# Attention with the probabilities as the stationary operand, V's two parts and a column of ones moving

## The chip, the cores and the metric

The kernel runs on one core of one Trainium2 chip. The metric is the device time of one execution in microseconds (us); shorter is better. Engines are named as in the profile: PE is TensorE's matmul, PEld its weight load (the load of the stationary operand), DVE is VectorE, ACT is ScalarE, POOL is GpSimd, SP issues most DMAs.

## The reference

Two layers of an encoder trunk run on a prompt of 1024 tokens and on a running stream of 32 tokens (float32, model width 1024). Layer 0 is forgetting attention with 16 heads of 64 features, layer 1 a gated linear recurrence; each is followed by a squared-ReLU MLP of 4096 hidden features. The part that matters here is the attention of the prompt:

```python
def fox_attend(q, k, v, cq, ck, qpos, kpos):
    logits = jnp.einsum('bqhd,bkhd->bhqk', q, k).astype(jnp.float32) * FOX_SCALE
    bias = jnp.swapaxes(cq, 1, 2)[..., :, None] - jnp.swapaxes(ck, 1, 2)[..., None, :]
    mask = kpos[None, :] <= qpos[:, None]
    logits = jnp.where(mask, logits + bias, -jnp.inf)
    p = jax.nn.softmax(logits, axis=-1).astype(v.dtype)
    return jnp.einsum('bhqk,bkhd->bqhd', p, v)
```

The mask is causal, so of the 8 x 8 blocks of 128 queries and 128 keys 36 are computed per head. The result is multiplied by a sigmoid gate and projected.

## The kernel before

Activations lie with features on partitions and tokens along the free axis, in three chunks of 352 tokens. Products keep float32 accuracy by splitting each operand exactly into a high and a low float32r part and adding three of the four products (`mm3`, line 152).

Heads are worked in eight pairs. For each pair `fox` (lines 639 to 648) calls `fox_attend` and then the projections of the next pair: V (`pj`, 72 matmuls of 352 columns), K, then `rest`, which turns V and K back to tokens on partitions (`to`, line 767), projects Q and writes the operands of the next attention. The tiles `vT`, `kh`, `qh` (features of a pair) and `KA`, `KB`, `QA`, `QX`, `VH`, `VL` (operands of the two heads) exist once, so each waits until the pair before has let go of it.

`fox_attend` has two parts. First, for both heads, the row maxima: 20 matmuls `mp` per head (line 835), each reduced by DVE (lines 840 and 843); the maxima are turned (`mt`, line 848) and go by DMA into a row of `QX`. Then per head, for two chunks of 512 queries and for each block of 128 keys: the logits `st` with keys on partitions and queries along the free axis (lines 866, 867; up to 512 columns), `pf` = exp on ACT (869), the causal triangle on POOL (871, on diagonal blocks), the high part `ph` on POOL (875), the low part `pl` on DVE (876), and three matmuls into `pv` (878 to 880) with a block of V stationary and the probabilities moving. `VH` holds V's high part in 64 columns and ones in the other 64, so that rows 64 to 127 of `pv` are the softmax's sums; `VL` holds the low part and zeros. ACT makes 1/sum by Ln and Exp, DVE multiplies, and the result, which has features on partitions, goes to DRAM.

The order of the work is made when the program is built: a list scheduler with a model of the engines places each instruction, and every engine then runs its own list in that order. The order of allocation binds it: of PSUM, tag A (projections, two banks), B (logits and maxima, three), E (`pv`, two) and D (one bank, for all that is turned on PE, `mt` and `to` among it) are handed on from tile to tile in the order of the program text.

Of the kernel before, what the change touches and what calls it, by code (L numbers as in the profile page):

```python
# [16 lines left out]
D = 1024  # L17
# [12 lines left out]
FMIN = 1e-15  # L30
TABLE = "natural_log_exp_and_others"


def consts():
# [11 lines left out]
    # pairs of key s and query t: in one block of four, then in the two halves of larger blocks  # L46
# [13 lines left out]
class K:  # L60
# [21 lines left out]
    def gains(self):  # L82
        # gains, features of a tile on partitions: loaded in rows, turned on the tensor engine
# [9 lines left out]
    # constants that the first products do not need  # L93
# [11 lines left out]
    # what frees PSUM goes ahead of other work  # L105
# [3 lines left out]
    # an order of two instructions on one engine  # L109
# [11 lines left out]
    # one unit of weights: [128, X, Y] with X*Y = 1024, split exactly into two float32r parts  # L121
# [29 lines left out]
    # out += W^T x over the given k tiles; each product in three float32r passes  # L151
# [12 lines left out]
    # per token of a chunk, tokens on partitions in three columns (the last one overlaps the  # L164
    # second): sums over all features of s, [128, C]
# [8 lines left out]
    # such columns as rows along the free axis, the same on every partition  # L174
# [7 lines left out]
    # running sum over feature tiles of y ** 2: [128, C], features of a tile on partitions  # L182
# [13 lines left out]
    # r = (ss / n + eps) ** -0.5  # L196
    def rsqrt(self, r, ss, n, pool):
# [9 lines left out]
        # one Newton step  # L207
# [13 lines left out]
    # x * gain in split form; y is scratch  # L221
# [13 lines left out]
    # the norm's factor per token, which the products take on later: as columns, or as rows  # L235
    def prestat(self, x, y, rows):
# [13 lines left out]
        # the product's factor is the square, which the norm after it takes to the square again  # L250
# [4 lines left out]
    # the norm's factor per token of y * sc, for y; ss the sums of y ** 2  # L255
# [14 lines left out]
    # x += rmsnorm(y * sc), sc a factor per token, acc the sum of y ** 2; y is overwritten  # L270
# [52 lines left out]
    # the last chunk of the output is normed with tokens on partitions, in three blocks (the last  # L323
    # one overlaps the second). Ahead of that: x in that form, and the gains on diagonals
# [43 lines left out]
    # one token chunk of the input: loaded with tokens on partitions,  # L368
# [11 lines left out]
    # brought to features on partitions, with the first norm's factor per token,  # L380
    def start_turn(self, n, pool, xts, tags):
# [36 lines left out]
    # normed and split  # L418
# [14 lines left out]
    # mixer's output (features on partitions, split, per token chunk) -> W_out -> norms ->  # L433
    # squared-ReLU MLP -> norms; returns the next layer's h, or writes the outputs
    def tail(self, os, w_out, layer, rs=None, after=None):
# [5 lines left out]
        with ExitStack() as c:  # L441
# [10 lines left out]
            # output projection  # L452
# [3 lines left out]
            # a factor of the norm before the products is less urgent than the next chunk's norms  # L456
# [24 lines left out]
            # MLP, G tiles of the hidden layer at a time  # L481
# [27 lines left out]
            # one output tile of the second matrix, over the given hidden tiles  # L509
# [27 lines left out]
            # the first three tiles of the hidden layer token chunk by token chunk, as the norms finish  # L537
# [25 lines left out]
            # the last two groups token chunk by token chunk, so that the norms overlap the products;  # L563
            # the last group's second weights in an h tile that is free by then
# [27 lines left out]
    # forgetting attention; returns its gated output  # L592
    def fox(self):
# [7 lines left out]
        with ExitStack() as c:  # L601
# [3 lines left out]
            # the input, token chunk by token chunk, with the first products on each  # L605
# [5 lines left out]
            tags = ("QA0", "QA1", "QX0", "QX1", "KA0", "KA1", "KB0", "KB1", "VH0", "VH1", "VL0", "VL1")  # L611
# [40 lines left out]
    # the forget gates of one token chunk: heads on partitions, tokens along the free axis  # L652
# [13 lines left out]
    def fox_setup(self, pool, psp, lf):  # L666
# [13 lines left out]
        # -cumulative sums; the scan runs on -logf  # L680
# [13 lines left out]
        # the same for the running streams, behind their cache  # L694
# [9 lines left out]
        # persistent operands of the two heads of a pair; rows 64.. carry the bias terms  # L704
# [4 lines left out]
        z64 = pool.tile([128, 64], F32, name="z64")  # L709
        self.v.memset(z64, 0.0)  # L710
        self.KA, self.KB, self.QA, self.QX, self.VH, self.VL = [], [], [], [], [], []
        for h in range(2):
            mk = lambda nm: pool.tile([128, SEQ], F32R, name=f"{nm}{h}", tag=f"{nm}{h}", bufs=1)
            ka, kb, qa, qx, vh, vl = (mk(nm) for nm in ("KA", "KB", "QA", "QX", "VH", "VL"))
            vh, vl = (t.rearrange("p (b f) -> p b f", b=8) for t in (vh, vl))
# [5 lines left out]
            self.VH.append(vh); self.VL.append(vl)  # L721

    # projections of one pair of heads: features on partitions
    def fox_pair(self, pool, psp, hs, w_in, p):
# [34 lines left out]
        def tok_out(src, dst_p, dst_s, keep):  # L759
            # back to tokens on partitions  # L760
# [18 lines left out]
        def keep_v(b0, tk):  # L779
            if b0 == 8:  # L780
                return
            for h in range(2):
                hi, lo = self.VH[h], self.VL[h]
                f = slice(64 * h, 64 * h + 64)
                self.v.tensor_copy(hi[:, b0:b0 + 4, 0:64], tk[:, :, f])
                self.v.tensor_tensor(lo[:, b0:b0 + 4, 0:64], tk[:, :, f], hi[:, b0:b0 + 4, 0:64].bitcast(F32), op=ALU.subtract)
# [34 lines left out]
    def fox_attend(self, pool, psp, p, cur, od):  # L821
        nc = self.nc
        qh = cur
        for h in range(2):
            r = slice(64 * h, 64 * h + 64)
            head = 2 * p + h
            ka, kb, qa, qx, vh, vl = self.KA[h], self.KB[h], self.QA[h], self.QX[h], self.VH[h], self.VL[h]
            # row maxima of the biased logits
# [23 lines left out]
            self.v.tensor_tensor(qx[0:64], qh[r, 0:SEQ], qa[r].bitcast(F32), op=ALU.subtract)  # L852
        for h in range(2):
            r = slice(64 * h, 64 * h + 64)
            head = 2 * p + h
            ka, kb, qa, qx, vh, vl = self.KA[h], self.KB[h], self.QA[h], self.QX[h], self.VH[h], self.VL[h]
            for c in range(2):
                pv = psp.tile([128, 512], F32, name=f"pv{head}_{c}", tag="E", bufs=2)
                nkb = 4 * c + 4
                for b in range(nkb):  # L860
                    q0 = max(512 * c, 128 * b)
                    N = 512 * c + 512 - q0
# [3 lines left out]
                    nc.tensor.matmul(ps[:, :N], lhsT=ka[:, kk], rhs=qa[:, q0:q0 + N], start=True, stop=False)  # L866
                    nc.tensor.matmul(ps[:, :N], lhsT=kb[0:97, kk], rhs=qx[0:97, q0:q0 + N], start=False, stop=True)  # L867
                    pf = pool.tile([128, 512], F32, name=f"pf{u}", tag="pf", bufs=3)
                    self.s.activation(pf[:, :N], ps[:, :N], AF.Exp, bias=self.ncol[:, b, head:head + 1])  # L869
                    if b >= 4 * c:  # L870
# [6 lines left out]
                    o = pv[:, q0 - 512 * c:]  # L877
# [441 lines left out]
```

## Time and profile before

| | |
|---|---|
| time, three runs | 2998.22 to 3001.53 us, median 3000.46 us |
| span of the profiled execution | 2996.0 us |
| PE busy over the span | 2942.2 us (98%), 18511 matmuls |
| PEld busy | 2855.2 us (95%) |
| DVE, ACT, POOL busy | 1734.0, 934.1, 967.0 us (58%, 31%, 32%) |
| first and last `pv` matmul | 136.2 and 682.2 us |

The execution that was profiled has no time of its own on record beside its span; the median of the runs is 4.5 us above the span, and this is taken as what lies around it. A busy time counts from an instruction's start to its modelled end; matmuls overlap, so 200 busy matmuls of 0.4 us can take far less than 80 us. The granted clock of TensorE is shown in tenths of full speed (9 stands for 90% or more) and is 9 in all 40 slices.

### The profile page before, as it was taken

What the parts mean: (1) busy time and instruction counts of PE and PEld (TensorE: products, weight loads), DVE (VectorE), ACT (ScalarE), POOL (GpSimd) and SP (SyncE); (2) the same over time, 40 slices, a digit from 0 to 9 for tenths busy, and PEclk for the clock granted to TensorE, in tenths of its full rate; (3) what the DMA queues carried; (4) which work ended last, traced back from release to release, by engine and by line L of the source; (5) the groups of instructions that cost most, each with busy time, mean ns of one, the idle gap of its engine ahead of it and who ended that gap; (6) DMA issues with size and microseconds to landing.
All of it is one profiled execution on the core that took longest, in us unless ns stands there. A gap on an engine that the chain in (4) does not pass through costs nothing.

```text
span 2996.0 us, 46448 instructions
## 1 busy us (share of the span) xinstructions
PE 2942.2 (98%) x18511; PEld 2855.2 (95%) x18511; DVE 1734.0 (58%) x2980; ACT 934.1 (31%) x1915; POOL 967.0 (32%) x1151
## 2 busy tenths in 40 slices
PE   7999999999999999999998999999999999999999
PEld 6888888899999999999997999999999999999998
DVE  6788888874544444445468656654474454454545
ACT  5455555555432111111133122212353111111112
POOL 3345444531432112121145444433362121121223
PEclk9999999999999999999999999999999999999999
DMA  5221121134321111121122111104432111111112
GB/s 152 62 52 44 48 53 48 51 112 147 106 74 57 43 43 50 36 57 49 37 82 95 35 59 41 47 27 120 140 118 76 36 57 43 43 50 36 57 61 69
DMA packets 217817, 195.59 MB, mean 65 GB/s; under 512 B 14312, under 2 KB 193648, under 8 KB 217472
## 3 DMA queue, kind: packets, MB, share of 16 engines
q1 hardware_dynamic: 216576, 192.49, 21.5%
q8 instruction: 145, 2.38, 0.3%
q14 instruction: 72, 0.59, 0.1%
q0 software_dynamic: 1024, 0.13, 0.0%
HBM read 147.00 MB, written 45.52 MB: 64 GB/s over the span
## 4 chain that ended last, share of the span: by engine, by line
PE 89%; DVE 5%; issue 1%; POOL 1%; ACT 1%; DMA 1%; SPq 0%; DVEq 0%; POOLq 0%; ACTq 0%
PE up L158 24%; PE dn L158 24%; PE hj L158 8%; PE pj L158 8%; PE gp L158 6%; PE po L158 5%; PE lv L1166 1%; PE ss L753 1%; PE pv L880 1%; PE pv L879 1%; PE pv L878 1%; PE st L867 1%; PE st L866 1%; PE mp L835 1%; PE lv L1181 1%
## 5 line engine op out<-in xcount | busy, mean ns | idle before, releaser
L520 DVE TENSOR_TENSOR ya<-dn,ya 128x352 f32<-128x352 f32 x672 | 348.3, 522 | 550.4 <-PE dn L158 550.4
L162 POOL TENSOR_TENSOR rl<-rl 128x352 f32<-128x352 f32 x192 | 190.2, 999 | 1031.7 <-ACT uh L501 1029.3
L145 DVE TENSOR_TENSOR wl<-wr,wh 128x1024 fp32r<-128x1024 f32 x203 | 280.4, 1382 | 147.0 <-ACT wh L142 84.6
L158 PE MATMUL dn<-uh,wl 128*128 128x352 f32 x1440 | 356.9, 323 | 0.0
L158 PE MATMUL dn<-uh,wh 128*128 128x352 f32 x1440 | 353.7, 324 | 2.5 <-DVE ya L520 2.5
L158 PE MATMUL dn<-ul,wh 128*128 128x352 f32 x1440 | 353.5, 323 | 0.0
L499 ACT ACTIVATE rl<-up 128x352 f32<-128x352 f32 x192 | 88.8, 463 | 783.1 <-PE up L158 712.8
L158 PE MATMUL up<-hh,wl 128*128 128x352 f32 x1536 | 291.5, 323 | 0.0
L158 PE MATMUL up<-hh,wh 128*128 128x352 f32 x1536 | 287.5, 323 | 2.1 <-ACT wh L142 1.7
L158 PE MATMUL up<-hl,wh 128*128 128x352 f32 x1536 | 288.1, 323 | 0.0
L158 PEld LDWEIGHTS up<-hh,wh 128*128 128x128 f32 x1536 | 253.5, 188 | 3.1 <-ACT wh L142 2.3
L158 PEld LDWEIGHTS dn<-uh,wh 128*128 128x128 f32 x1440 | 251.3, 188 | 4.4 <-DVE ya L520 4.4
L158 PEld LDWEIGHTS up<-hh,wl 128*128 128x128 f32 x1536 | 254.4, 188 | 0.0
L158 PEld LDWEIGHTS up<-hl,wh 128*128 128x128 f32 x1536 | 254.1, 188 | 0.0
L158 PEld LDWEIGHTS dn<-uh,wl 128*128 128x128 f32 x1440 | 252.6, 188 | 0.0
L158 PEld LDWEIGHTS dn<-ul,wh 128*128 128x128 f32 x1440 | 251.8, 188 | 0.0
L144 POOL TENSOR_SCALAR wh<-wr 128x1024 fp32r<-128x1024 f32 x109 | 120.8, 1108 | 294.3 <-PE pj L158 93.0
L503 DVE TENSOR_TENSOR ul<-rl,uh 128x352 fp32r<-128x352 f32 x192 | 142.6, 754 | 124.9 <-POOL rl L162 124.8
L142 ACT CAST wh<-wr 128x1024 fp32r<-128x1024 f32 x94 | 98.7, 1050 | 347.2 <-PE up L158 221.5
L876 DVE TENSOR_TENSOR pl<-pf,ph 128x512 fp32r<-128x512 f32 x192 | 124.5, 652 | 59.9 <-POOL ph L875 34.7
L875 POOL TENSOR_SCALAR ph<-pf 128x512 fp32r<-128x512 f32 x192 | 125.2, 654 | 51.6 <-PE pv L879 24.7
L869 ACT ACTIVATE pf<-st,ncol 128x512 f32<-128x512 f32 x192 | 109.7, 578 | 71.2 <-PE st L867 40.1
(343 smaller groups left out, 5673.0 us busy)
## 6 DMA issues: line engine op xcount, KB each, us to landing
wr<-in_ffn_w_up_dram SPq DMA_DIRECT2D x64, 512.0 KB, 4.0
wr<-in_ffn_w_down_dram SPq DMA_DIRECT2D x64, 512.0 KB, 3.8
wr<-in_fox_w_in_dram SPq DMA_DIRECT2D x32, 512.0 KB, 4.1
wr<-in_hgrn_w_in_dram SPq DMA_DIRECT2D x32, 512.0 KB, 4.1
x<-xd SPq DMA_DIRECT2D x22, 704.0 KB, 4.9
xd<-x SPq DMA_DIRECT2D x18, 704.0 KB, 3.1
out_dram<-tk SPq DMA_DIRECT2D x32, 256.0 KB, 2.4
odg<-go SPq DMA_DIRECT2D x30, 176.0 KB, 2.5
```

The source lines that it names most:

```text
L142: self.s.copy(wh, raw)
L144: self.g.tensor_scalar(out=wh, in0=raw, scalar1=1.0, scalar2=0.0, op0=ALU.mult, op1=ALU.add)
L145: self.v.tensor_tensor(wl, raw, wh.bitcast(F32), op=ALU.subtract)
L158: self.nc.tensor.matmul(ps, lhsT=ws[kk][a], rhs=xs[kk][b], start=i == 0, stop=i == tot - 1)
L162: self.g.tensor_tensor(out, a, b, op=op)
L499: self.s.activation(rl, ps[:, :C], AF.Relu)
L503: self.v.tensor_tensor(ul, rl, uh.bitcast(F32), op=ALU.subtract)
L520: self.v.tensor_tensor(ys[n][:, o], ps[:, :C], ys[n][:, o], op=ALU.add)
L753: nc.tensor.matmul(ss[:, :C], lhsT=self.blk, rhs=sq, start=True, stop=True)
L869: self.s.activation(pf[:, :N], ps[:, :N], AF.Exp, bias=self.ncol[:, b, head:head + 1])
L875: self.g.tensor_scalar(out=ph[:, :N], in0=pf[:, :N], scalar1=1.0, scalar2=0.0, op0=ALU.mult, op1=ALU.add)
L876: self.v.tensor_tensor(pl[:, :N], pf[:, :N], ph[:, :N].bitcast(F32), op=ALU.subtract)
```

## The change

The product of probabilities and V is turned round: a 128 x 128 block of probabilities is stationary and V moves. One tile `VV` per head holds, for each block of keys, V's low part (64 columns), its high part (64) and two columns of ones. `ph` meets all 130 columns, `pl` the last 66; the output `pv` has queries on partitions, three blocks of queries side by side in one bank. The queries are therefore taken in three chunks of 3, 3 and 2 blocks in place of two of 4, so `st`, `pf`, `ph` and `pl` have at most 384 columns. Per chunk DVE takes the reciprocal of the ones column, ACT copies the low columns out, DVE adds the high ones and multiplies into `oq` (two buffers, by the pair's parity). When the second head of a pair is far enough, eight blocks of `oq` are turned on PE (`ot`, PSUM tag D), copied by ACT and sent to DRAM. The Ln and Exp of the sums and the tile of zeros are gone. The rest of the difference is comments and line numbers.

```diff
+VW = 130
...
-                jk = pool.tile([128, 512], F32, name=f"jk{t0}_{hf}", tag="w", bufs=1)
+                jk = pool.tile([128, 512], F32, name=f"jk{t0}_{hf}", tag="oT", bufs=2)
...
-            tags = ("QA0", "QA1", "QX0", "QX1", "KA0", "KA1", "KB0", "KB1", "VH0", "VH1", "VL0", "VL1")
+            tags = ("QA0", "QA1", "QX0", "QX1", "KA0", "KA1", "KB0", "KB1", "VV0", "VV1", "oq0", "oq1")
...
-            self.g.tensor_copy(vh[:, :, 64:128], self.ones[:, None, 0:64].to_broadcast([128, 8, 64]))
-            self.g.tensor_copy(vl[:, :, 64:128], z64[:, None, :].to_broadcast([128, 8, 64]))
...
+            vv = pool.tile([128, 8, VW], F32R, name=f"VV{h}", tag=f"VV{h}", bufs=1)
...
+            self.g.tensor_copy(vv[:, :, 128:VW], self.ones[:, None, 0:VW - 128].to_broadcast([128, 8, VW - 128]))
...
+        oq = pool.tile([128, 8, 128], F32, name=f"oq{p}", tag=f"oq{p % 2}", bufs=1)
         for h in range(2):
...
-            for c in range(2):
-                nkb = 4 * c + 4
-                for b in range(nkb):
+            for c0, c1 in ((0, 3), (3, 6), (6, 8)):
...
+                pv = pv[:, 0:3 * VW].rearrange("p (i f) -> p i f", f=VW)
+                for b in range(c1):
...
-                    nc.tensor.matmul(o, lhsT=vh[:, b], rhs=ph[:, :N], start=b == 0, stop=False)
-                    nc.tensor.matmul(o, lhsT=vl[:, b], rhs=ph[:, :N], start=False, stop=False)
-                    nc.tensor.matmul(o, lhsT=vh[:, b], rhs=pl[:, :N], start=False, stop=b == nkb - 1)
...
-                self.s.activation(w[r], pv[64:128], AF.Ln)
-                self.s.activation(w[r], w[r], AF.Exp, scale=-1.0)
...
-                self.v.tensor_tensor(oT[r], pv[0:64], w[r], op=ALU.mult)
-                nc.sync.dma_start(od[p][r, qc], oT[r])
+                    for t, f0 in ((ph, 0), (pl, 64)):
+                        for i in range(q0, c1):
+                            nc.tensor.matmul(pv[:, i - c0, f0:VW], lhsT=t[:, (i - q0) * 128:(i - q0) * 128 + 128],
+                                             rhs=vv[:, b, f0:], start=b == f0 == 0 and i == c0,
+                                             stop=b == i or b == f0 == 0, skip_group_check=b + f0 > 0 or i > c0)
...
+                self.v.reciprocal(rc, pv[:, 0:nq, 128])
...
+                with self.soon():
+                    self.s.copy(lo, pv[:, 0:nq, 0:64])
+                    self.v.tensor_tensor(lo, pv[:, 0:nq, 64:128], lo, op=ALU.add)
+                self.v.tensor_tensor(oq[:, c0:c1, r], lo, rc[:, :, None].to_broadcast([128, nq, 64]), op=ALU.mult)
+                if h and c0:
+                    a, b = (0, 4) if c0 == 3 else (4, 8)
+                    ps = psp.tile([128, 512], F32, name=f"ot{u}", tag="D", bufs=1)
+                    for i in range(a, b):
+                        nc.tensor.transpose(ps[:, (i - a) * 128:(i - a) * 128 + 128], oq[:, i], self.ident)
...
+                    self.s.copy(oT, ps)
+                    nc.sync.dma_start(od[p][:, a * 128:b * 128], oT)
```

Two places on PE show what becomes of the order. In a name the first number counts: `pv3_0` is head 3 (the second of pair 1) and the chunk of queries that starts at 0, `vT2` belongs to pair 2; a number after that is the tile's own. The first place is the start of head 3's product. Before:

```order
L878 MATMUL pv3_0_2244<-ph232_2251,VH1_864 128x512
L879 MATMUL pv3_0_2244<-ph232_2251,VL1_865 128x512
L753 MATMUL ss274_2763<-sq274_2760,mats_261 128x352
L158 MATMUL pj351_3272<-hh7_227,wh350_3268 128x352 x8
L158 MATMUL pj351_3272<-hh7_227,wl350_3269 128x352 x4
L880 MATMUL pv3_0_2244<-pl232_2252,VH1_864 128x512
L866 MATMUL st238_2316<-QA1_862,KA1_860 128x512
L867 MATMUL st238_2316<-QX1_863,KB1_861 128x512
```

And now, at the same head:

```order
L882 MATMUL pv3_0_2520<-VV1_860,ph241_2527 128x130 x3
L882 MATMUL pv3_0_2520<-VV1_860,pl241_2528 128x66 x3
L868 MATMUL st246_2600<-QA1_858,KA1_856 128x384
L869 MATMUL st246_2600<-QX1_859,KB1_857 128x384
L882 MATMUL pv3_0_2520<-VV1_860,ph242_2543 128x130 x2
L882 MATMUL pv3_0_2520<-VV1_860,pl242_2544 128x66 x2
L868 MATMUL st247_2615<-QA1_858,KA1_856 128x384
L869 MATMUL st247_2615<-QX1_859,KB1_857 128x384
```

Three matmuls of 512 columns became six of 130 and 66, and the projections (`pj`, of pair 3's V) that stood between the steps of this head before are not there now.

The second place is the end of the same head, where the maxima of pair 2 begin. Before:

```order
L880 MATMUL pv3_1_2303<-pl244_2398,VH1_864 128x128
L767 MATMUL to276_2773<-ident_70,kh2_2411 128x128 x2
L835 MATMUL mp290_2832<-KB0_851,QX0_853 128x512
L158 MATMUL pj353_3324<-hh39_664,wh350_3268 128x352 x3
L158 MATMUL pj353_3324<-hl39_665,wh350_3268 128x352 x3
L835 MATMUL mp291_2835<-KB0_851,QX0_853 128x128
L158 MATMUL pj353_3324<-hl39_665,wh350_3268 128x352 x5
L158 MATMUL pj355_3356<-hh7_227,wh354_3352 128x352 x2
L835 MATMUL mp293_2839<-KB0_851,QX0_853 128x512
L158 MATMUL pj355_3356<-hh7_227,wh354_3352 128x352 x6
```

Now:

```order
L898 MATMUL ot257_2782<-ident_70,oq1_2265 128x128 x2
L833 MATMUL mp311_3235<-KB0_849,QX0_851 128x512
L833 MATMUL mp312_3238<-KB0_849,QX0_851 128x512
L833 MATMUL mp314_3253<-KB1_857,QX1_859 128x128
L765 MATMUL to272_3000<-ident_70,vT2_2790 128x128 x4
L833 MATMUL mp316_3257<-KB1_857,QX1_859 128x256
L833 MATMUL mp318_3262<-KB1_857,QX1_859 128x384
L765 MATMUL to274_3012<-ident_70,vT2_2790 128x128 x4
L833 MATMUL mp320_3267<-KB1_857,QX1_859 128x512
L765 MATMUL to276_3024<-ident_70,vT2_2790 32x128
L833 MATMUL mp322_3272<-KB1_857,QX1_859 128x512
L159 MATMUL pj371_3897<-hh39_664,wh368_3841 128x352 x8
```

Before, the turning of `vT2` lay far ahead of this point, at the start of pair 1's attention. Now it comes after `ot`, whose bank D it needs, and the next projection `pj371` (the last third of pair 3's V) comes after that, since `vT` exists once.

## Rows read from the trace of the kernel before

**Rows 1.** The page: PE's share of the span, and the chain that ended last.

```profile
PE 2942.2 (98%) x18511; PEld 2855.2 (95%) x18511; DVE 1734.0 (58%) x2980; ACT 934.1 (31%) x1915; POOL 967.0 (32%) x1151
PE 89%; DVE 5%; issue 1%; POOL 1%; ACT 1%; DMA 1%; SPq 0%; DVEq 0%; POOLq 0%; ACTq 0%
```

**Rows 2.** Busy time by engine, 120 to 640 us: PE, PEld, DVE, ACT, POOL, clock, DMA.

```profile
120.00:640.00 520.00, 513.25 (x2941) 463.25 (x2939) 432.64 (x939) 277.22 (x558) 237.47 (x397) 1.00 0.21 55
```

**Rows 3.** Groups by shape, 100 to 690 us, line 878: count | busy, mean ns.

```profile
L878 PE MATMUL pv<-ph,VH 128*128 128x512 f32 x96 | 38.5, 401 | 1.3 <-POOL ph L875 1.3
L878 PE MATMUL pv<-ph,VH 128*128 128x384 f32 x32 | 10.8, 338 | 0.0
L878 PE MATMUL pv<-ph,VH 128*128 128x256 f32 x32 | 8.9, 279 | 0.0
L878 PE MATMUL pv<-ph,VH 128*128 128x128 f32 x32 | 7.5, 235 | 0.0
```

**Rows 4.** Timeline of weight loads, 133.5 to 135.3 us: start, duration, what.

```profile
133.75 0.19 PEld L867 LDWEIGHTS st<-QX,KB 97*128 97x128 f32 x1
133.93 0.69 PEld L158 LDWEIGHTS pj<-hl,wh 128*128 128x128 f32 x4
...
134.86 0.19 PEld L866 LDWEIGHTS st<-QA,KA 128*128 128x128 f32 x1
134.98 0.19 PEld L867 LDWEIGHTS st<-QX,KB 97*128 97x128 f32 x1
135.09 0.19 PEld L866 LDWEIGHTS st<-QA,KA 128*128 128x128 f32 x1
135.21 0.19 PEld L867 LDWEIGHTS st<-QX,KB 97*128 97x128 f32 x1
```

**Rows 5.** The same, 306.9 to 308.2 us.

```profile
307.13 0.19 PEld L879 LDWEIGHTS pv<-ph,VL 128*128 128x128 f32 x1
307.36 0.19 PEld L880 LDWEIGHTS pv<-pl,VH 128*128 128x128 f32 x1
```

**Rows 6.** The same, 1687 to 1689.5 us: the recurrence's products of 64 columns.

```profile
1687.30 2.07 PEld L1166 LDWEIGHTS lv<-q,k 128*128 128x128 f32 x18
```

**Rows 7.** The same, 255 to 275 us: four 128 x 128 blocks turned.

```profile
254.93 0.52 PEld L767 LDWEIGHTS to<-ident,kh 128*128 128x128 f32 x4
```

**Rows 8.** Groups by shape, 100 to 690 us: DVE in the attention.

```profile
L876 DVE TENSOR_TENSOR pl<-pf,ph 128x384 fp32r<-128x384 f32 x32 | 19.1, 597 | 5.2 <-POOL ph L875 4.0 <-ACT gz L910 0.9
L876 DVE TENSOR_TENSOR pl<-pf,ph 128x256 fp32r<-128x256 f32 x32 | 17.3, 540 | 8.3 <-POOL ph L875 4.6 <-PE pv L880 3.0 <-ACT pf L869 0.7
L876 DVE TENSOR_TENSOR pl<-pf,ph 128x128 fp32r<-128x128 f32 x32 | 11.4, 356 | 5.3 <-PE pv L880 5.2
L840 DVE TENSOR_REDUCE mx<-mp 128x1 f32<-128x512 f32 x64 | 44.0, 687 | 6.2 <-PE mp L835 5.6
L840 DVE TENSOR_REDUCE mx<-mp 128x1 f32<-128x384 f32 x32 | 17.7, 552 | 5.6 <-PE mp L835 5.2
L840 DVE TENSOR_REDUCE mx<-mp 128x1 f32<-128x256 f32 x32 | 13.4, 418 | 3.5 <-PE mp L835 3.5
L840 DVE TENSOR_REDUCE mx<-mp 128x1 f32<-128x128 f32 x32 | 9.0, 282 | 0.5 <-PE mp L835 0.2
L843 DVE CUSTOM_DVE_ANT_0 jk<-mp,mats 128x128 f32<-128x128 f32 x128 | 36.0, 281 | 3.9 <-PE mp L835 3.0
L843 DVE DVE_READ_ACCUMULATOR2_ANT mx<- 128x1 f32 x128 | 10.5, 82 | 0.0
L805 DVE CAST KB<-kh 64x1024 fp32r<-64x1024 f32 x14 | 11.7, 838 | 0.2
L807 DVE TENSOR_TENSOR KA<-kh,KA 64x1024 fp32r<-64x1024 f32 x14 | 17.8, 1269 | 0.4
L809 DVE CAST QX<-qh 64x1024 fp32r<-64x1024 f32 x16 | 18.1, 1131 | 0.2
L852 DVE TENSOR_TENSOR QX<-qh,QA 64x1024 fp32r<-64x1024 f32 x16 | 19.5, 1219 | 0.2
```

More of the change, by code (lines that the diff above doesn't have):

```diff
@@ L708, in fox_setup @@
         self.v.memset(aux[64:65, 1:2], 1.0)
-        z64 = pool.tile([128, 64], F32, name="z64")
-        self.v.memset(z64, 0.0)
-        self.KA, self.KB, self.QA, self.QX, self.VH, self.VL = [], [], [], [], [], []
+        self.KA, self.KB, self.QA, self.QX, self.VV = [], [], [], [], []
         for h in range(2):
             mk = lambda nm: pool.tile([128, SEQ], F32R, name=f"{nm}{h}", tag=f"{nm}{h}", bufs=1)
-            ka, kb, qa, qx, vh, vl = (mk(nm) for nm in ("KA", "KB", "QA", "QX", "VH", "VL"))
-            vh, vl = (t.rearrange("p (b f) -> p b f", b=8) for t in (vh, vl))
+            ka, kb, qa, qx = (mk(nm) for nm in ("KA", "KB", "QA", "QX"))
+            vv = pool.tile([128, 8, VW], F32R, name=f"VV{h}", tag=f"VV{h}", bufs=1)
             self.g.tensor_copy(kb[64:128], aux[64:128, 0:1].to_broadcast([64, SEQ]))
             self.g.tensor_copy(qx[64:128], aux[64:128, 1:2].to_broadcast([64, SEQ]))
-            self.g.tensor_copy(vh[:, :, 64:128], self.ones[:, None, 0:64].to_broadcast([128, 8, 64]))
-            self.g.tensor_copy(vl[:, :, 64:128], z64[:, None, :].to_broadcast([128, 8, 64]))
+            self.g.tensor_copy(vv[:, :, 128:VW], self.ones[:, None, 0:VW - 128].to_broadcast([128, 8, VW - 128]))
             self.KA.append(ka); self.KB.append(kb); self.QA.append(qa); self.QX.append(qx)
-            self.VH.append(vh); self.VL.append(vl)
+            self.VV.append(vv)
     def fox_pair(self, pool, psp, hs, w_in, p):
@@ L782, in keep_v @@
             for h in range(2):
-                hi, lo = self.VH[h], self.VL[h]
+                lo, hi = (self.VV[h][:, b0:b0 + 4, a:a + 64] for a in (0, 64))
                 f = slice(64 * h, 64 * h + 64)
-                self.v.tensor_copy(hi[:, b0:b0 + 4, 0:64], tk[:, :, f])
-                self.v.tensor_tensor(lo[:, b0:b0 + 4, 0:64], tk[:, :, f], hi[:, b0:b0 + 4, 0:64].bitcast(F32), op=ALU.subtract)
+                self.v.tensor_copy(hi, tk[:, :, f])
+                self.v.tensor_tensor(lo, tk[:, :, f], hi.bitcast(F32), op=ALU.subtract)
         def outs(nm):
@@ L855, in fox_attend @@
             head = 2 * p + h
-            ka, kb, qa, qx, vh, vl = self.KA[h], self.KB[h], self.QA[h], self.QX[h], self.VH[h], self.VL[h]
-            for c in range(2):
-                pv = psp.tile([128, 512], F32, name=f"pv{head}_{c}", tag="E", bufs=2)
-                nkb = 4 * c + 4
-                for b in range(nkb):
-                    q0 = max(512 * c, 128 * b)
-                    N = 512 * c + 512 - q0
+            ka, kb, qa, qx, vv = self.KA[h], self.KB[h], self.QA[h], self.QX[h], self.VV[h]
+            for c0, c1 in ((0, 3), (3, 6), (6, 8)):
+                pv = psp.tile([128, 512], F32, name=f"pv{head}_{c0}", tag="E", bufs=2)
+                pv = pv[:, 0:3 * VW].rearrange("p (i f) -> p i f", f=VW)
+                for b in range(c1):
+                    q0 = max(c0, b)
+                    N = (c1 - q0) * 128
                     u = self.uid()
@@ L865, in fox_attend @@
                     kk = slice(b * 128, b * 128 + 128)
-                    nc.tensor.matmul(ps[:, :N], lhsT=ka[:, kk], rhs=qa[:, q0:q0 + N], start=True, stop=False)
-                    nc.tensor.matmul(ps[:, :N], lhsT=kb[0:97, kk], rhs=qx[0:97, q0:q0 + N], start=False, stop=True)
+                    qs = slice(q0 * 128, c1 * 128)
+                    nc.tensor.matmul(ps[:, :N], lhsT=ka[:, kk], rhs=qa[:, qs], start=True, stop=False)
+                    nc.tensor.matmul(ps[:, :N], lhsT=kb[0:97, kk], rhs=qx[0:97, qs], start=False, stop=True)
                     pf = pool.tile([128, 512], F32, name=f"pf{u}", tag="pf", bufs=3)
                     self.s.activation(pf[:, :N], ps[:, :N], AF.Exp, bias=self.ncol[:, b, head:head + 1])
-                    if b >= 4 * c:
+                    if b >= c0:
                         self.g.affine_select(out=pf[:, 0:128], in_=pf[:, 0:128], pattern=[[1, 128]],
@@ new lines, in fox_attend @@
+                nq = c1 - c0
+                rc = pool.tile([128, 4], F32, name=f"rc{u}", tag="rc", bufs=2)[:, 0:nq]
+                self.v.reciprocal(rc, pv[:, 0:nq, 128])
+                lo = pool.tile([128, 3, 64], F32, name=f"w{u}", tag="w", bufs=2)[:, 0:nq]
+                with self.soon():
+                    self.s.copy(lo, pv[:, 0:nq, 0:64])
+                    self.v.tensor_tensor(lo, pv[:, 0:nq, 64:128], lo, op=ALU.add)
+                self.v.tensor_tensor(oq[:, c0:c1, r], lo, rc[:, :, None].to_broadcast([128, nq, 64]), op=ALU.mult)
@@ new lines, in fox_attend @@
+                if h and c0:
[3 more added lines that the diff above has]
+                        nc.tensor.transpose(ps[:, (i - a) * 128:(i - a) * 128 + 128], oq[:, i], self.ident)
+                    oT = pool.tile([128, 512], F32, name=f"oT{u}", tag="oT", bufs=2)
+                    self.s.copy(oT, ps)
+                    nc.sync.dma_start(od[p][:, a * 128:b * 128], oT)
```

7 lines of the change are left out of this document (1 added, 6 removed).

## Prediction

> **What bounds the kernel now.** I read the page's shares and its chain of waits first: PE is busy 98% of the span and makes up 89% of the chain [rows 1]. A busy PE overstates itself, so the next view is the table of stretches: from 120 to 640 us, the attention, PE is busy 513 of 520 us, DVE 433, ACT 277, POOL 237 [rows 2]. So in this stage PE's list is what takes the time, DVE is second with 87 us free, and the other two have half their time free. A change here is priced first by what it does to PE's list, then by whether DVE can still keep up at each place.
>
> The third view says what a matmul costs there. A matmul's own duration is a latency, not a rate. The starts of the weight loads give the rate, because a load starts when the matmul before it takes over the array. After the load at 307.13 a matmul of 512 columns runs until the next load at 307.36: 0.23 us [rows 5]. In the same way 384 columns take 0.18 (133.75 to 133.93; I use 0.175, which fits 512 in proportion), 256 columns 0.12, and 128 columns 0.11 and 0.12 [rows 4]. The last two are the point: from 512 to 256 the time halves with the columns, from 256 to 128 it does not. The recurrence shows it in a longer series: 18 loads of 128 x 128 for products of only 64 columns take 2.07 us, that is (2.07 - 0.19)/17 = 0.111 us each [rows 6]. A matmul with a fresh 128 x 128 stationary operand costs the larger of 0.45 ns a column and 0.11 us.
>
> **The change part by part.** *The product with V.* Before, line 878 has 96 matmuls of 512 columns and 32 each of 384, 256 and 128 [rows 3], and lines 879 and 880 have as many. 3 x (96 x 0.23 + 32 x 0.175 + 32 x 0.12 + 32 x 0.11) = 105 us. After, each of the 36 blocks of a head needs two matmuls, one of 130 columns and one of 66, each with its own stationary block: 16 x 36 x 2 = 1152, all under the 0.11 us that a load takes: 127 us. The columns fall from 221,000 to 113,000, but the time rises by 22 us.
>
> Rows 6 bear on a rule that speaks otherwise. The Trainium skill, "TensorE: Matmul & The Clock Gate", section "Back-to-back issue gap", gives some 81 ns for a load and a matmul of 128 columns in a stream; by that figure the 1152 would take an estimated 93 us and the term would be -12 us. The trace does not agree for these operands (0.111 us).
>
> *The logits.* Chunks of 3, 3 and 2 blocks keep the 4608 columns of a head but cut them into 17 pieces in place of 12: per line 80 of 384, 144 of 256, 48 of 128 against 96, 32, 32, 32. Two lines: 73.2 against 70.1, +3 us.
>
> *Turning back.* 64 blocks of 128 x 128. Four such take 0.52 us from the first load's start to the last one's end [rows 7], about 0.12 each with the next one: +7.7 us.
>
> PE's list grows by 22 + 3 + 8 = 32 us (bounds: 0.11 or 0.12 for every short matmul, 30 to 45). Nothing hides it, for PE is the bound.
>
> *Other engines.* DVE gets 80 more subtractions with the same columns in all; their fixed part is 0.17 us (0.356 for 128 columns, 0.540 for 256 [rows 8]), 14 us. It gets 48 times a reciprocal, an add and a multiply over 128 to 192 columns, which the trace does not show; by the rows of 128 and 256 columns between 0.36 and 0.54 for each of the large two and 0.17 for the small one; I take the lower end, 0.9 together: 43 us, less the 32 multiplies that go. That fits the 87 free us on average. ACT loses Ln and Exp and gets copies, POOL gets 80 more casts of smaller size: cost nothing, their 243 and 283 free us hide them. If that cover were gone, it would show as waits for `ph`, which is in the third rival. Fewer and larger stores to DRAM, the tags at the start and the smaller set-up: nothing, they are beside PE's first products.
>
> *Where the order leaves PE without projections.* This is the term that the averages miss. `ot` takes bank D after the whole product; the turning of the next pair's V is behind it in D; `vT` is therefore freed only then, and of the pair after next only two of three V projections can be on the two banks A. The second head of pairs 1, 3 and 5 and the maxima behind it then stand on PE with no projection between. In that stretch PE's list has 29 `st` (8 of 384, 16 of 256, 5 of 128), 78 products, 17 turned blocks and 17 `mp` (8 of 512, 3 each of 384, 256, 128): 3.9 + 8.6 + 1.9 + 3.1 = 17.4 us. DVE's list for the same stretch has 5, 10 and 4 subtractions of 384, 256 and 128 columns (9.8 us), the maxima up to the one that frees the bank for the last `mp` (4, 2, 3 and 3 reductions of 512, 384, 256 and 128, and 10 diagonal ones at 0.281 + 0.082: 9.6 us), the casts KB, KA, QX and the late QX (0.84 + 1.27 + 1.13 + 1.22 = 4.5 us) and four normalisations (3.6 us): 27.5 us [rows 8]. The two lists wait for each other through three buffers, so the stretch takes DVE's time: 10.1 us of PE idle, three times. By the same count pair 0 has 10.0 us on PE against 20.9 (10 subtractions, all maxima and casts, two normalisations), pair 2 4.3 against 11.1, pair 4 4.0 against 9.1 (maxima and one normalisation); pairs 6 and 7 have gate products between. Sum 53 us. Its bounds are 0, if DVE comes to each stretch far enough ahead, and 53. Three buffers of `ph` and `pl` let it be about 1.8 us ahead, and PE's small waits elsewhere (513 of 520 is not full) shrink as the displaced projections are packed closer; I take off 3 us a stretch, 18 in all: 35 us.
>
> Sum against the profiled execution's span: 2996.0 + 32 + 35 = 3063 us; the median of the runs stands 4.5 us above that span, so 3067 us.
>
> **The rivals.** *Only the work counts* (24%). The stretches cost nothing, since DVE's list can be ahead and PE's slower short products give it time; PE stays the bound: 3000.5 + 32 = 3033, own range 3022 to 3046. For it speaks that PE waits only 7 us in the stage now; against it the sum of 27.5 against 17.4.
>
> *The stretches cost all, and more waits appear* (15%). The stationary operand is now what POOL and DVE have just made, so a load cannot be issued ahead of it. A load lasts 0.19 us and only 0.11 of it are in the rate [rows 4]; where PE waits for `ph` or `pl`, 0.08 more are laid open. There are 16 x 17 x 2 = 544 such groups; if half of them wait, 22 us. 32 + 53 + 22 = 107: 3107 us; own range 3090 to 3120.
>
> *The loads hide* (3%). If each load ran wholly under the matmul before it, 130 and 66 columns would cost 0.45 ns a column: 113,000 columns are 51 us, -54 us for the product, +11 for the rest, and with the projections still dense enough 2957: faster. It decides as soon as a short matmul costs under some 0.08 us, where the sum of PE's terms crosses zero. Rows 4 and 6 speak against it; for it only that loads do run under matmuls of 256 columns and more. The Trainium skill, in the page on TensorE named above, section "Step-by-step: what each phase is for", says that the next tile's weights load while this tile's matmul runs; the trace agrees from 256 columns up and not below.
>
> *No change that can be measured* (3%): some half-hidden load with part of the stretches.
>
> **How the numbers follow.** The forecast holds 55%, own range 3046 to 3090, likeliest 3067. What a measurement of this kernel can tell from no change is about 0.2%, 6 us. Faster 3%, same 3%, slower 94%. The range from 3026 to 3100 leaves out the two small cases, two thirds of the third rival and the lowest tail of the first.
>
> **What would show it.** After: starts of loads 0.11 us apart in the series of 130 and 66 columns, and no closer; 1152 such loads. If they are 0.06 apart, the step on the load is wrong. In the second half of pairs 1, 3 and 5 a stretch of some 25 us in which PE's digits fall while DVE is busy nearly throughout, and in the list of waits `mp` waiting for DVE's maxima and `pv` for `pl`. If PE is as full there as elsewhere, the step on the order is wrong and the time near 3033. The last matmul of the product with V, which starts at 682 us now, should start near 750. After the attention nothing should differ. The forecast fails upward if the waits for `ph` are many and short.

## The result, and the profile after

The changed kernel takes 3092.36 us (median of five runs, 3088.83 to 3092.73) against 3000.08 for the kernel before in the same session: 1.031 times as long, 95% interval 1.0295 to 1.032. That is 92 us more; 67 were forecast. The time lies in the stated range of 3026 to 3100, but 2 us above the forecast's own 3046 to 3090.

The page of the changed kernel, its line of PE and its chain [rows 1]:

```profile
PE 3015.4 (98%) x19311; PEld 2939.4 (95%) x19311; DVE 1761.0 (57%) x3171; ACT 933.8 (30%) x1995; POOL 972.5 (31%) x1229
PE 91%; DVE 6%; ACT 1%; issue 1%; DMA 1%; POOL 0%; SPq 0%; DVEq 0%; ACTq 0%; POOLq 0%
```

These shares do not show the loss: PE is as "full" as before. The page's row of clock digits has one 8 (the fourth slice) where before all were 9. The table of stretches tells it; its columns are as in [rows 2], and the number behind the five engines is the granted clock:

```profile
183.00:196.00 13.00, 12.25 (x37) 9.28 (x38) 12.35 (x47) 3.08 (x7) 0.78 (x3) 0.50 0.20 65
196.00:245.00 49.00, 47.32 (x296) 43.75 (x296) 28.60 (x62) 20.84 (x54) 13.61 (x27) 1.00 0.19 51
245.00:268.00 23.00, 21.94 (x174) 21.62 (x172) 19.47 (x40) 15.11 (x31) 18.14 (x36) 1.00 0.00 1
268.00:285.00 17.00, 15.72 (x49) 12.26 (x50) 14.75 (x55) 3.13 (x8) 2.05 (x4) 0.50 0.19 65
285.00:310.00 25.00, 23.71 (x145) 22.16 (x144) 14.91 (x33) 10.14 (x24) 6.82 (x12) 1.00 0.24 65
606.00:619.00 13.00, 11.67 (x35) 8.71 (x36) 12.89 (x51) 3.08 (x7) 0.31 (x2) 0.50 0.20 64
```

At the end of pair 0 (183 to 196 us), pair 1 (268 to 285) and pair 5 (606 to 619) DVE is busy for 87 to 99% of the stretch, PE starts few matmuls (37 in 13 us, where the 49 us before 245 have 296), and the granted clock is 0.50, TensorE's lower level of 1.2 GHz. Pair 3 ends like them. The ends of pairs 2 and 4 are shorter: 10 us at 0.50 each, with DVE busy for 69 and 65%, and about half of that time falls on the projections behind. In all there are six stretches of 10 to 17 us, 78 us together. From 120 to 640 us the kernel before had a mean clock of 1.00 [rows 2]. In the last row PE is "busy" 11.67 of 13 us, since a matmul's modelled end lies later at the lower clock: the busy share hides the loss, the count of matmuls shows it.

The timeline of PE through the end of pair 1 (start, duration, instruction; in brackets the idle time before it and who ended it):

```profile
266.79 0.41 PE L882 MATMUL pv<-VV,pl 128*128 128x66 f32 x2 [0.27 <-DVE pl L878]
268.65 1.12 PE L833 MATMUL mp<-KB,QX 96*128 96x384 f32 x2 [1.45 <-DVE mx L841]
...
270.53 0.77 PE L833 MATMUL mp<-KB,QX 96*128 96x512 f32 x1
...
276.20 1.07 PE L765 MATMUL to<-ident,vT 128*128 128x128 f32 x4
...
280.67 2.71 PE L159 MATMUL pj<-hh,wh 128*128 128x352 f32 x8
283.19 2.36 PE L159 MATMUL pj<-hh,wl 128*128 128x352 f32 x8
285.38 1.45 PE L159 MATMUL pj<-hl,wh 128*128 128x352 f32 x8
286.67 0.81 PE L159 MATMUL pj<-hh,wh 128*128 128x352 f32 x4
```

From 254.0 to 280.7 us there is no projection: 26.6 us (27.5 was DVE's list, 3 off for a lead). PE waits 1.45 us, until 268.65, for the maxima's readers (`mx`); within this wait, at 268.1, the granted clock falls. When the projections come back at 280.67, nothing holds them, and yet eight take 2.5 us from start to start (280.67 to 283.19), at the full clock 1.3 (285.38 to 286.67): that is the clock alone.

The waits of PE from 120 to 740 us (total, times, longest):

```profile
PE mp L833 <- DVE mx L841: 9.2, 10, 1.7
PE ss L751 <- ACT sq L749: 7.3, 13, 0.8
PE to L765 <- ACT tk L767: 1.2, 5, 0.2
PE mp L833 <- DVE mx L838: 1.2, 3, 0.7
PE pv L882 <- DVE pl L878: 0.8, 3, 0.3
PE pj L159 <- ACT vT L741: 0.5, 1, 0.5
PE pv L882 <- POOL ph L877: 0.5, 1, 0.5
```

**Where the 92 us are.** I price every interval between the starts of two weight loads, up to the MLP's first matmul: the matmul's rate (0.45 ns a column, at least 0.111 us) is work; what an interval takes above it while the granted clock is at half, up to once more the rate, is clock; the rest is wait.

| us up to the MLP | work | clock | wait |
|---|---|---|---|
| before | 738.9 | 2.7 | 71.2 |
| after | 767.0 | 28.7 | 106.9 |
| difference | 28 | 26 | 36 |

Together 90 us; behind that point the two profiled executions differ by 5 us. The split depends on how intervals a little shorter than the rate are counted: with the bare rates, each interval priced by the matmul that runs in it, the differences are 32, 27 and 31, so each of the three is good to some 5 us. Work was forecast at 32, the starved stretches at 35, the clock not at all. Since the rate is the prediction's own, the column of work does not test it; the spacing of the loads does, below. The half-clock stretches of the attention last 78 us; the border between clock and wait is soft: 12 of the 26 us fall on projections and gate products, which wait for nothing (as at 280.67 above); the rest nearly all on matmuls inside the stretches, where PE would else have spent part of that time waiting for DVE.

### The profile page after: what moved, and what is told of

Read it like the earlier page. It is cut to its first block, busy times and chain, and to the rows that moved or that the text cites. A ratio compares the mean times of both kernels' runs of the same rounds, so it can differ in the third digit from the quotient of the medians.

```text
span 3090.9 us, 48534 instructions
## 1 busy us (share of the span) xinstructions
PE 3015.4 (98%) x19311; PEld 2939.4 (95%) x19311; DVE 1761.0 (57%) x3171; ACT 933.8 (30%) x1995; POOL 972.5 (31%) x1229
## 4 chain that ended last, share of the span: by engine, by line
PE 91%; DVE 6%; ACT 1%; issue 1%; DMA 1%; POOL 0%; SPq 0%; DVEq 0%; ACTq 0%; POOLq 0%
PE up L159 23%; PE dn L159 23%; PE pj L159 9%; PE hj L159 8%; PE gp L159 6%; PE po L159 6%; PE pv L882 3%; PE lv L1179 1%; PE st L868 1%; PE st L869 1%; PE ss L751 1%; PE mp L833 1%; PE to L765 1%; PE lv L1194 1%; PE pS L1223 1%
## 5 line engine op out<-in xcount | busy, mean ns | idle before, releaser
L146 DVE TENSOR_TENSOR wl<-wr,wh 128x1024 fp32r<-128x1024 f32 x203 | 280.7, 1383 | 149.4 <-ACT wh L143 84.7
L159 PEld LDWEIGHTS up<-hl,wh 128*128 128x128 f32 x1536 | 254.0, 188 | 0.0
L504 DVE TENSOR_TENSOR ul<-rl,uh 128x352 fp32r<-128x352 f32 x192 | 149.1, 788 | 125.2 <-POOL rl L163 125.1
L878 DVE TENSOR_TENSOR pl<-pf,ph 128x256 fp32r<-128x256 f32 (+2 forms) x272 | 138.9, 523 | 60.0 <-POOL ph L877 40.5
L877 POOL TENSOR_SCALAR ph<-pf 128x256 fp32r<-128x256 f32 (+2 forms) x272 | 143.3, 533 | 87.3 <-PE pv L882 54.0
L871 ACT ACTIVATE pf<-st,ncol 128x256 f32<-128x256 f32 (+2 forms) x272 | 127.0, 486 | 109.4 <-PE st L869 63.5
```

The costliest lines, as they stand in the source:

```text
L146: self.v.tensor_tensor(wl, raw, wh.bitcast(F32), op=ALU.subtract)
L159: self.nc.tensor.matmul(ps, lhsT=ws[kk][a], rhs=xs[kk][b], start=i == 0, stop=i == tot - 1)
L504: self.v.tensor_tensor(ul, rl, uh.bitcast(F32), op=ALU.subtract)
L877: self.g.tensor_scalar(out=ph[:, :N], in0=pf[:, :N], scalar1=1.0, scalar2=0.0, op0=ALU.mult, op1=ALU.add)
L878: self.v.tensor_tensor(pl[:, :N], pf[:, :N], ph[:, :N].bitcast(F32), op=ALU.subtract)
```

## The experiments

The theory under test: short products cost their load (28 us); the turn of the outputs (`ot`) in the one bank D ahead of the next pair's V starves PE of projections (36); the starved PE is granted half of the full clock (26). The rivals are in the expectations.

**The turn later.** The transposes of `oq` are moved from the end of `fox_attend` behind the next pair's `rest()`:

```diff
+                    self.fox_back(pool, psp, p, oq, od)     # behind pr.rest()
...
-                if h and c0:                                # in fox_attend
-                    a, b = (0, 4) if c0 == 3 else (4, 8)
-                    ps = psp.tile([128, 512], F32, name=f"ot{u}", tag="D", bufs=1)
```

> The changed kernel with one step moved: the transposes that turn the outputs back (ot, tag D) and their copies come in program order after the next pair's rest(), so after its V turning (to, tag D), in place of before it. Every matmul, transpose, copy and DMA is kept; in TensorE's order the long stretches without projections at the pair boundaries are gone (the largest that is left holds 8 us, 2.6 us of it projections). Theory (short products +28 us, projections starved behind the one D bank +36 us, granted clock at half there +26 us): both the 36 and the 26 go, apart from some 5 us at the stretches left, and 3000 + 28 + 2 to 8 gives 3030 to 3038 us, with a granted clock of 1.00 through the pairs 1 to 6. Rival A (the waits come from the product itself, whose stationary operand DVE and POOL make): the order doesn't matter, 3075 us or more. Rival B (the half clock comes from the short products and not from the idle time before it): the waits go, 36 us, the half clock stays: 3055 to 3062 us.

Measured 3050.7 us, 1.0169 (1.0154 to 1.0184): 42 us come back, the forecast had 54 to 62, so the time misses the theory's range by 13 us. Work 766.9, clock 9.4, wait 84.5. So 22 of the 36 and 19 of the 26 go, rival A (3075 or more) falls, and so does rival B: the short products are all there, and the clock stays up in the ends of pairs 0 to 2. What is left of the half clock sits in pairs 3 to 5, of the waits in pairs 2 to 5. Rows of its table of stretches:

```profile
120.00:240.00 120.00, 118.78 (x797) 112.19 (x795) 95.83 (x235) 60.05 (x141) 52.97 (x100) 1.00 0.15 44
240.00:310.00 70.00, 68.55 (x460) 64.41 (x459) 57.38 (x143) 33.39 (x76) 30.79 (x59) 1.00 0.16 47
...
470.00:550.00 80.00, 76.99 (x495) 71.60 (x495) 59.84 (x148) 37.28 (x88) 33.82 (x66) 0.96 0.16 45
```

**Another bank.** One word of the changed kernel:

```diff
-                    ps = psp.tile([128, 512], F32, name=f"ot{u}", tag="D", bufs=1)
+                    ps = psp.tile([128, 512], F32, name=f"ot{u}", tag="E", bufs=2)
```

> The changed kernel with one word changed: the tile in which the outputs are turned back has tag E (two PSUM banks) in place of D (one bank, which the turning of the next pair's V needs). The place in the program stays; in TensorE's order the long stretches without projections go as well. Theory: as with the late turn, 3030 to 3040 us and no half clock at the pair boundaries, since it is the one bank of D that holds the projections back. Rival A (the product itself waits): 3075 us or more. Rival C (it is not the bank but the transposes' place at the end of a head that holds TensorE): as after, 3085 to 3095 us.

Measured 3056.7 us, 1.0188 (1.0173 to 1.0203); work 766.5, clock 12.9, wait 87.2. A miss by 17 us, but rivals A and C fall: with the transposes in the same place of the program 36 us come back by the bank alone.

**Both cures.** The late turn, and its tile in E (both diffs above).

> The two cures together: the late turn of e1_turn_late and the tag E of e2_turn_bank_E. E1 ended 20 us above the 3030 of the bare sum (13 us of waits and 7 of half clock left in pairs 2 to 5), e2 26 us. Theory: with both, the turn of the outputs meets neither V's turn in D nor the start of the next product in E for long, the waits left fall to 0 to 8 us and the half clock to 0 to 4: 3030 to 3042 us. Rival (what is left in e1 and e2 is the product's own, since a stationary operand that DVE and POOL make can't be loaded ahead): 3045 to 3056 us as in those.

Measured 3042.4 us, 1.0144 (1.0129 to 1.0159); work 767.8, clock 10.4, wait 79.0. The time is 0.4 us above the theory's upper end and outside the rival's range: half of the changed kernel's loss is gone, and most of the rest is the work (29 us above before); 8 us of wait and 8 of clock stay above before's, where the theory had at most 4 of clock. What still waits longest are the maxima, not the product. From PE's waits, 120 to 740 us (before, `mp` waits 0.3 us for `mx`):

```profile
PE mp L837 <- DVE mx L845: 5.8, 8, 2.0
...
PE pv L886 <- POOL ph L881: 0.5, 1, 0.5
...
PE pv L886 <- DVE pl L882: 0.3, 1, 0.3
```

**The turn alone, in the kernel before.** Its product with V stays in 512 moving columns; behind each chunk of a second head:

```diff
+                if h:
+                    ps = psp.tile([128, 512], F32, name=f"ot{u}", tag="D", bufs=1)
+                    for i in range(4):
+                        nc.tensor.transpose(ps[:, i * 64:i * 64 + 64], oT[r, i * 128:i * 128 + 128], self.ident[r, r])
+                    ow = pool.tile([128, 512], F32, name=f"ow{u}", tag="oT", bufs=2)
+                    self.s.copy(ow[:, 0:256], ps[:, 0:256])
```

> The kernel before, its product with V unchanged (512 moving columns), plus a turn through the bank D at the place where the changed kernel has one: behind each chunk of a pair's second head four 64-row transposes of oT into a tile of tag D and a ScalarE copy of 256 columns to scratch that nothing reads. It adds 64 transposes of some 0.1 us, 7 us of TensorE work. Theory: the order then leaves TensorE without projections at the ends of the pairs 1, 3, 5 (10.9 us of work there, where VectorE has some 20 us) and a little at the others, so of the 36 us of waits a third to a half, 12 to 18, and of the half clock some 5 to 26: 3025 to 3050 us. Rival A (the product with the short matmuls makes the waits): nothing but the 7 us, 3005 to 3010 us.

Measured 3050.3 us, 1.0168 (1.0153 to 1.0184): 50 us for 64 small transposes. Work is 742.6 (3.7 more, not 7), clock 19.9 (17 more), wait 103.6 (32 more). The time is 0.3 us above the theory's range; the waits, forecast at 12 to 18, are twice that. Rival A falls: the waits and the half clock don't need the short products. Three ends of pairs, in its table of stretches:

```profile
257.00:271.00 14.00, 13.33 (x42) 9.83 (x42) 12.05 (x44) 3.71 (x8) 0.12 (x1) 0.52 0.18 49
414.00:428.00 14.00, 13.54 (x42) 9.97 (x43) 12.70 (x47) 3.71 (x8) 0.12 (x1) 0.52 0.19 52
574.00:588.00 14.00, 13.45 (x43) 9.76 (x43) 12.34 (x45) 3.71 (x8) 0.12 (x1) 0.51 0.18 49
```

**Its control.** The same kernel with the added tile in E in place of D, nothing else.

> The control of e4_before_turn_D: the same kernel before with the same added turn of oT (64 transposes, copies to scratch that nothing reads), with tag E in place of D and nothing else changed. Theory: the +50 us of e4 were the place in bank D, so here the work of the 64 transposes is left, 4 to 7 us, and a few us of waits, 3004 to 3020 us, with no half clock at the pair boundaries. Rival A (a turn of the outputs costs this much wherever it is put, as it waits for DVE's mult at a head's end): 3040 to 3052 us.

Measured 3024.0 us, 1.0079 (1.0064 to 1.0094): the letter of the bank is worth 26 us. It is 4 us above what the theory gave: work 742.8, clock 7.8, wait 80.2, so a turn in E costs some 14 us of waits and clock too. These transposes load 64 partitions, not 128, and start closer than 0.11 us: a load lasts 0.14, so the four of this row start (0.33 - 0.14)/3 = 0.06 us apart; that fits added work of less than 7 us.

```profile
263.43 0.33 PEld L892 LDWEIGHTS ot<-ident,oT 64*128 64x128 f32 x4 [0.31 <-issue]
```

From 120 to 740 us, the turn in D and then the turn in E:

```profile
120.00:740.00 620.00, 597.10 (x3286) 530.47 (x3285) 456.89 (x979) 312.86 (x629) 262.10 (x438) 0.96 0.20 54
```

```profile
120.00:740.00 620.00, 606.88 (x3491) 550.51 (x3490) 480.58 (x1012) 333.70 (x671) 268.16 (x444) 0.99 0.22 61
```

**More columns, the same loads.** On the late turn, `pl` meets all 130 columns:

```diff
-                                             rhs=vv[:, b, f0:], start=b == f0 == 0 and i == c0,
+                                             rhs=vv[:, b], start=b == k == 0 and i == c0,
```

> The kernel with the late turn (e1_turn_late) with the low part pl also meeting all 130 columns: the moving columns of 576 short matmuls go from 66 to 130, 36.9 thousand columns more, the number of loads stays 1152. Theory (a short matmul costs its load of 0.11 us, whatever it moves): loads of pl stand 0.11 us apart as before, the work stays within 3 us, and the time within 3045 to 3056 us (e1 had 3050.7; the order around it differs a little). Rival B (the columns set the price, 0.45 ns for one as in the 512-column matmuls): 16.6 us more, 3062 to 3070 us.

**Fewer columns, the same loads.** Both parts meet the last 66 (`vv[:, b, 64:]`).

> The other way: both parts of the probabilities meet 66 columns alone (V's first part and the ones), 36.9 thousand columns fewer than in e1_turn_late, the same 1152 loads. It leaves out the product of ph with V's second part (64 columns that the output then takes a second time from the first part). Theory: loads of ph and pl both stand 0.11 us apart, work within 3 us of e1, 3043 to 3056 us. Rival B: 16.6 us less, 3030 to 3036 us.

Measured 3046.0 us (1.0156, 1.0141 to 1.0171) and 3044.7 us (1.0154, 1.0137 to 1.0171). From 66 to 130 columns for both parts, 74,000 columns more, the time moves by 1 us, where rival B has 33. Both lie some 5 us under the late turn's 3050.7, whose columns are between theirs; that the order around the product makes these 5 us is argued, not tried. The weight loads in the timelines of the changed kernel (130 columns for `ph`, 66 for `pl`), of both at 130, and of both at 66 (start, duration of the row, count):

```profile
257.97 0.41 PEld L882 LDWEIGHTS pv<-VV,pl 128*128 128x128 f32 x3
...
258.53 0.41 PEld L882 LDWEIGHTS pv<-VV,ph 128*128 128x128 f32 x3
```

```profile
262.96 0.30 PEld L886 LDWEIGHTS pv<-VV,pl 128*128 128x128 f32 x2
263.18 0.30 PEld L886 LDWEIGHTS pv<-VV,ph 128*128 128x128 f32 x2
263.40 0.30 PEld L886 LDWEIGHTS pv<-VV,pl 128*128 128x128 f32 x2
```

```profile
263.18 0.30 PEld L886 LDWEIGHTS pv<-VV,pl 128*128 128x128 f32 x2 [0.99 <-DVE pl L882]
263.40 0.19 PEld L886 LDWEIGHTS pv<-VV,ph 128*128 128x128 f32 x1
```

A load lasts 0.19, so three in 0.41 us start (0.41 - 0.19)/2 = 0.11 us apart, two in 0.30 us as well; from 262.96 to 263.40 four loads take 0.44. Over the whole attention of the changed kernel, at full clock, the median from one load to the next is 0.111 us for the products of 66 columns and 0.112 for those of 130. The price doesn't ask for the columns.

**The clock: maxima twice.**

```diff
-                    nc.tensor.matmul(ps[:, :w], lhsT=qx[0:96, qb * 128:(qb + 1) * 128], rhs=kb[0:96, c0:c0 + w],
+                    for _ in range(2 if w == 512 and 0 < p < 7 else 1):
+                        nc.tensor.matmul(ps[:, :w], lhsT=qx[0:96, qb * 128:(qb + 1) * 128], rhs=kb[0:96, c0:c0 + w],
```

> The changed kernel with the 512-column matmuls of the row maxima (mp) issued twice in the pairs 1 to 6, the second writing the same values again: 6 x 12 matmuls of 0.23 us, 16.6 us more TensorE work, nearly all of it within the stretches where TensorE waits for VectorE. Theory: the stretches' length is set by VectorE and stays, so the work itself costs 0 to 6 us there; if it keeps TensorE busy enough for the granted clock to stay at 1.00, up to 26 us come back: 3066 to 3092 us, each stretch kept at full clock being worth some 4 us. Rival D (the half clock costs nothing, as TensorE waits there anyway): 3092 to 3100 us whatever the clock does; if the clock still falls to 0.50 in all six stretches, the run tells only that the extra work is covered (3090 to 3100).

Measured 3084.0 us, 1.0279 (1.0262 to 1.0296): 8 us faster than the changed kernel with 18 us more work (784.8); clock 21.3, wait 87.0. That is inside the theory's range and outside rival D's 3092 to 3100. Work put into the waits costs nothing there; that the time falls below the changed kernel's needs something else that got shorter, and the half clock did. At the ends of pairs 2 and 4 the clock no longer falls. These two, in the changed kernel and then with the maxima twice:

```profile
345.00:375.00 30.00, 27.95 (x144) 23.91 (x143) 22.63 (x71) 9.17 (x19) 7.06 (x14) 0.83 0.21 65
512.00:542.00 30.00, 28.36 (x148) 25.08 (x147) 22.86 (x68) 9.21 (x17) 8.56 (x15) 0.83 0.22 64
```

```profile
340.00:370.00 30.00, 28.66 (x179) 26.15 (x178) 24.81 (x72) 11.04 (x20) 8.91 (x15) 1.00 0.29 90
505.00:535.00 30.00, 28.85 (x177) 26.02 (x176) 24.55 (x71) 10.71 (x20) 8.99 (x15) 1.00 0.27 82
```

In 30 us 179 and 177 matmuls start in place of 144 and 148. From one pair's first `pv` to the next one's, with the projections that changed pairs taken off at 0.16 us each, pairs 2 and 4 are 4.0 and 2.6 us shorter than in the changed kernel. The four pairs at whose ends the clock still fell, for 3 to 7 us less than before, are between 0.8 us shorter and 0.4 longer.

**The clock: four times, at three ends.** As before, with `range(4 if w == 512 and p in (2, 4, 6) else 1)`.

> The clock by itself: the changed kernel with the 512-column maxima matmuls of the pairs 2, 4 and 6 issued four times (the same values written again), 25 us more TensorE work. In TensorE's order the three long stretches at the ends of the pairs 1, 3, 5 stay where they were and hold 23.1 us of work in place of 17.6 (VectorE has 27 us there), so 16.5 us of it lie in waits and 8 us outside them; the stretches at the ends of the pairs 0, 2, 4 are untouched and serve as control. Theory (TensorE's idle time makes the granted clock fall, and the half clock lengthens the kernel by about 4 to 5 us a boundary): at the three filled boundaries the clock stays at 1.00 or falls for a shorter time, 8 to 13 us come back, and the time is 3084 to 3093 us in spite of 25 us more work; at the three control boundaries the clock falls as before. Rival D (the half clock costs nothing, as TensorE waits for VectorE there): 3099 to 3104 us, the 8 us outside the waits, whatever the clock does. Rival E (the extra matmuls lengthen the stretches, since a repeat sits between VectorE's reads): over 3105 us.

Measured 3104.6 us, 1.0353 (1.0339 to 1.0367): a miss by 12 us, at the upper edge of rival D (3099 to 3104), so that the time alone doesn't speak against D here. Work 793.3, clock 25.8, wait 93.4. The filling was too thick for the test: once the clock falls, four matmuls of 512 columns between two of DVE's reads take 4 x 0.43 us, and PE itself sets the pace. At the three control ends the clock fell as before (0.50 for 17, 7 and 7 us). Of the filled ends, only at the end of pair 1 did the clock stay up for most of the stretch; the ends of pairs 1, 3 and 5:

```profile
268.00:285.00 17.00, 14.39 (x66) 11.42 (x67) 15.07 (x54) 4.47 (x10) 3.28 (x6) 0.90 0.19 63
...
438.00:452.00 14.00, 13.40 (x48) 10.99 (x49) 9.92 (x33) 1.44 (x3) 1.60 (x3) 0.64 0.10 38
...
606.00:619.00 13.00, 11.28 (x40) 9.37 (x40) 9.34 (x28) 2.65 (x5) 4.09 (x6) 0.61 0.06 20
```

From one pair's first `pv` to the next one's, pair 1 takes 77.5 us (78.9 in the changed kernel), pairs 3 and 5 take 79.8 and 80.0 (74.4 and 74.7). These are not like for like: 18 projections and two other matmuls of 352 columns, 3.2 us, have left pair 1. With them the same edit costs +1.8 us where the clock held for most of the stretch and +5.4 where it fell. That agrees with a price of the half clock, but three places of one execution settle no size.

## Why the prediction was right, and what it missed

Two of the three causes were forecast, and nearly at their size; the third, the half clock, was not. That the stated range still holds the time is partly luck: 3092 lies outside the forecast's own range, and the room above 3090 was there for the third rival, whose mechanism did not come.

- *A short matmul costs its load, 0.11 us.* Right, and shown: the spacing of the loads, and no difference between 66 and 130 columns. The work came to 28 us (32 by the bare rates) for 32. It holds for loads of 128 x 128; the loads of 64 partitions in the control start 0.06 us apart. The rival in which loads hide fell with it. The Trainium skill, "TensorE: Matmul & The Clock Gate", section "Weight-path perf modes — Fast Weight Load (FWL) and DoubleRow", says that the fast load of weights is not for FP32 inputs; the 0.11 us do not contradict it, but no run here has another type of operand.
- *DVE's normalisations, 43 us.* They measure 44 us (reciprocals 8, adds 16, multiplies 21). Over the whole attention DVE has room for them; that they cost only inside the stretches is argued, not tried.
- *`ot` in bank D starves PE of projections.* Right and shown three ways: by the place in the program, by the bank in the changed kernel, by the bank in the kernel before. The waits are 36 us for the 35 forecast, but not where they were forecast. From one pair's first `pv` to the next, waits and clock together grow by 12, 10, 10, 9, 9 and 9 us for pairs 0 to 5, 59 us; the forecast had 8, 7, 4, 7, 2 and 7. The ends of pairs 1, 3 and 5 got 28 for 21, those of pairs 0, 2 and 4 31 for 14.
- *The step that failed* is "so the stretch takes DVE's time: 10.1 us of PE idle, three times". It took the idle time as all that a stretch costs. In each of the six ends the granted clock fell to 0.50 as well, and the projections behind ran at half speed: a term of 12 to 26 us was missing. The run with the maxima twice gives 2.6 and 4.0 us for the two ends of 10 us at which the clock held. The rows of before show no such stretch in the attention, since PE is dense there; but a term that has PE stand idle for 10 us in 27 had to ask whether PE's rate stays what those rows say. The Trainium skill has the rule, in "TensorE: Matmul & The Clock Gate", section "HAM oscillation — how this bites in real kernels": a kernel whose matmuls keep waiting falls to the lower clock each time and pays half of the throttled time. By that rule the 78 us at 0.50 are an estimated 39 us. The trace agrees on the fall and has less for the price, 12 to 26 us, as part of the slower matmuls stands in the place of waiting.
- *The third rival's waits for `ph` and `pl`* (22 us) did not come: in the whole execution the product's matmuls wait 4.7 us for both, in the kernel before 6.4. The time came into this rival's own range of 3090 to 3120 for another reason.
- *The last product with V* starts at 788 us; 750 was forecast. Of these 38 us some 17 are 109 gate products of 0.16 us that now stand ahead of it. *After the attention nothing differs*: all but 5 us lie ahead of the MLP's first matmul.
- *Open:* how the 26 us divide between clock and wait, and why 16 us of waits and clock stay with both cures (14 in the control with E), though most of the waits that stay are at the maxima; that any added turn at a pair's end holds projections up a little is argued, not tried. No variant here beats the kernel before: the 28 us of loads stay in all with the turned product.

## What to carry to other kernels

Count the loads, not the columns, when an operand becomes stationary in small blocks: with a 128 x 128 stationary block and 66 to 130 moving columns a matmul here costs 0.11 us whatever it moves. When a new tile joins a PSUM tag with one bank, look whose turn in that bank comes behind it: 64 small transposes cost 50 us in one tag and 23 in another. And where a change leaves TensorE idle for some 10 us at a time, add to the idle time what the work behind it costs at half the clock.

## What the hardware showed that was not expected

The granted clock fell to half in each of the six ends of pairs in which PE waited for DVE, for 10 to 17 us, and stayed there for the first projections behind them: eight in 2.5 us in place of 1.3. With the maxima issued twice it stayed at 1.00 at two of these ends, where 35 and 29 more matmuls started in 30 us, and still fell at the other four. A PE share of 90% in such a stretch (11.67 of 13 us) goes with 35 matmuls, 0.37 us each from start to start on the mean, against 0.17 in the 49 us from 196 to 245.
